# The last product of a two-block network over the listed experts in place of all 16384

## The chip, the cores and the metric

One Trainium2 chip, one core. The metric is the device time of one execution in microseconds (us); lower is better. Engines: PE (TensorE matmul) and PEld (its weight load), DVE (VectorE), ACT (ScalarE), POOL (GpSimd), SP (which here only issues DMAs). PEq, ACTq, SPq and POOLq are the sequencers of these engines.

## The reference

Two transformer blocks on 256 tokens of width 2048, all float32. The first is a convolution mixer and a gated feed-forward; the second is attention with a pooling branch, and then "peer", a layer that picks single-neuron experts. The change concerns only peer:

```
q = (xt @ w_query).reshape(t, 8, 256)            # t = 256 tokens, 8 heads
s1, s2 = q1 . sub_keys_1, q2 . sub_keys_2        # 128 scores each
v1, i1 = top_k(s1, 16);  v2, i2 = top_k(s2, 16)
cand = v1[:, None] + v2[None, :];  top_s, top_pos = top_k(cand, 16)
expert_idx = i1 * 128 + i2 at top_pos;  gates = softmax(top_s)
a   = einsum('thkd,td->thk', expert_u[expert_idx], xb)
out = einsum('thk,thkd->td', gelu(a) * gates, expert_v[expert_idx])
```

So each token weighs 128 of 16384 experts (some may coincide). expert_u and expert_v are 16384 x 2048.

## The kernel before

The kernel doesn't gather. It takes the layer as dense products with a matrix of gates that is zero where an expert wasn't chosen. Expert number e is i * 128 + j, with i on the 128 partitions and j counted in rows of U: row j of the stream holds the experts i * 128 + j for all i. A "half" c is 128 of the 256 tokens.

**Precision.** Each product is three float32r matmuls: both operands are split in a high part (ACT, L69 for streamed weights, L193 for other tiles) and a low part (DVE, L84 and L194), and high x high, high x low and low x high are summed in PSUM.

**Weights.** SP loads all weights in tiles of 128 x 1024 (512 KB), in one order that `stream` writes down (L61). 4 raw tiles (`NRAW`) and 7 split tiles (`NHL`) are in flight; `tick`, called once a row, splits 5 tiles ahead (`LOOK`). A row of U is two such tiles.

**Side work.** `aside(cost, f)` puts work at the end of one list; each `tick` adds `budget` to a credit and takes side work off the front while credit is left.

**The stages of peer.** `query_stage` makes queries and scores and picks the top 16 (`choose`). 128 `gate_step`s, as side work with cost 2.0 at a budget of `BU` = 2.7 a row, each turn two tokens' choices into a 128 x 128 matrix of gates per token: one-hot rows (L1324, L1325) times gates (L1327) on PE (L1332), joined to tile `gch` (L1342). A `gch` of 16 tokens goes to DRAM `gd` by the ACT queue (L1345), 8 KB contiguous for a partition. Beside these, `expert_in` computes the 128 rows of gelu(a) (L187, L1354) and stores each to DRAM `ad`, 1 KB for a partition, again by the ACT queue (L1355); the tile it is stored from has 4 buffers. The last 8 rows (U2) are computed in `expert_out`.

**The last product.** `expert_out` loads gates and gelu(a) for 8 rows at a time (`gin`, L1371; `ain`, L1373; SP queue), multiplies (L1379) and splits them, and multiplies all 128 rows j with the split V, for both halves c and four quarters q of 512 columns: 128 x 2 x 4 x 3 matmuls of 512 columns (L1395 to L1397; some of the last are 256 wide). After each 8 rows `collect` adds the PSUM sums to `acc` in SBUF (L1402). The last sums go out by DMA.

Of the kernel before, what the change touches and what calls it, by code (L numbers as in the profile page):

```python
# [6 lines left out]
F32 = mybir.dt.float32  # L7
# [5 lines left out]
P = 128  # L13
D = 2048
# [23 lines left out]
CH, BU = 4, 2.7  # L38
U1 = 120
ENDS = (0, 0, 512), (1, 0, 256), (1, 256, 256)  # L40
# [55 lines left out]
class Kern:  # L96
    def __init__(self, ctx, tc, A, out):
        self.tc, self.nc, self.A, self.out = tc, tc.nc, A, out
        pool = lambda name, bufs, **k: ctx.enter_context(tc.tile_pool(name=name, bufs=bufs, **k))
        self.pool = pool  # L100
        self.cst = pool("cst", 1)
        self.wraw = pool("wraw", NRAW)
        self.whl = pool("whl", NHL)
        self.tmp = pool("tmp", 3)
        self.small = pool("small", 2)
        self.psA = pool("psA", 5, space=bass.MemoryType.PSUM)
        self.psB = pool("psB", 3, space=bass.MemoryType.PSUM)
# [3 lines left out]
        self.gd = self.dram.tile([P, 16, P, 16], F32, name="gd")  # L111
        self.ad = self.dram.tile([P, P, T], F32, name="ad")
# [175 lines left out]
    def stream(self):  # L288
# [44 lines left out]
        add("V", [A["V"][i] for i in range(P)])  # L333
# [375 lines left out]
    def run(self):  # L709
        nc, tc = self.nc, self.tc  # L710
        self.consts()
        self.stream()
        self.sq = self.cst.tile([P, T], F32, name="sq")
        self.r2 = self.cst.tile([P, T], F32, name="r2")
        silu = self.conv_stage()
        with ExitStack() as late:
            big = self.big = late.enter_context(tc.tile_pool(name="big", bufs=1, reuse_waits="tile"))
            self.ex = late.enter_context(tc.tile_pool(name="ex", bufs=1, reuse_waits="tile"))
            self.t2 = late.enter_context(tc.tile_pool(name="t2", bufs=2, reuse_waits="tile"))
            h = self.bp.tile([P, KD, T], F32, tag="B", name="h")  # L720
# [8 lines left out]
        with ExitStack() as ctx:  # L729
            self.pk = ctx.enter_context(tc.tile_pool(name="pk", bufs=1, reuse_waits="tile"))  # L730
            self.query_stage(xn)
            self.expert_in(xn)
            self.drain()
        self.expert_out(xn, acc)
# [474 lines left out]
    def query_stage(self, xn):  # L1209
        nc = self.nc  # L1210
        pk = self.pk
# [7 lines left out]
        self.sel = [pk.tile([P, 3, P], F32, name=f"sel{c}") for c in range(2)]  # L1219
# [37 lines left out]
    def choose(self, c, val, idx, top, pos, idf):  # L1257

        nc, pk = self.nc, self.pk
# [42 lines left out]
        def turn():  # L1302
# [3 lines left out]
            st = pk.tile([P, 3, P], F32, name=f"selT{c}")  # L1306
            nc.scalar.activation(st.rearrange("p w t -> p (w t)"), ps[:, :3 * P], AF.Copy)
            gh = pk.tile([P, 2, P], F32R, name=f"gh{c}")
# [7 lines left out]
    def gate_step(self, c, st, gh, t0):  # L1316

        nc, pk = self.nc, self.pk
        o1 = pk.tile([P, 2, P], F32R, tag="o1", name=self.nm("o1"), bufs=3)
        oh = pk.tile([P, 2, P], F32, tag="oh", name=self.nm("oh"), bufs=3)  # L1320
        o2 = pk.tile([P, 2, 2, P], F32R, tag="o2", name=self.nm("o2"), bufs=3)
        for u in range(2):
            t = t0 + u
            nc.vector.tensor_scalar(o1[:, u], self.iota, st[:, 0, t:t + 1], None, op0=ALU.is_equal)  # L1324
            nc.vector.tensor_scalar(oh[:, u], self.iota, st[:, 1, t:t + 1], None, op0=ALU.is_equal)  # L1325
            for w in range(2):
                nc.scalar.activation(o2[:, u, w], oh[:, u], AF.Copy, scale=gh[:, w, t:t + 1])  # L1327
# [8 lines left out]
        def ev(ps):  # L1336
            if t0 % 16 == 0:
                self.gch = pk.tile([P, P, 16], F32, tag="gch", name=self.nm("gch"), bufs=2)
# [3 lines left out]
            nc.vector.tensor_tensor(out=self.gch[:, :, t0 % 16:t0 % 16 + 2].rearrange("p j t -> p t j"),  # L1342
                                    in0=v[:, :, 0], in1=t, op=ALU.add)
# [4 lines left out]
    def expert_in(self, xn, second=False):  # L1348
        nc = self.nc

        def ev_a(j, ps):
# [3 lines left out]
            nc.scalar.dma_start(self.ad[j], t)  # L1355
# [6 lines left out]
    def expert_out(self, xn, acc):  # L1362
        nc, tc, W = self.nc, self.tc, self.W
        G = 8
        with ExitStack() as ctx:
            hp = ctx.enter_context(tc.tile_pool(name="hp", bufs=2, reuse_waits="tile"))
            gin, ain, hid = {}, {}, {}

            def load(g):
                gin[g] = hp.tile([P, 16, G, 16], F32, tag="gin", name=f"gin{g}")  # L1370
                nc.sync.dma_start(gin[g], self.gd[:, :, g * G:g * G + G])  # L1371
                ain[g] = hp.tile([P, G, T], F32, tag="ain", name=f"ain{g}")
                nc.sync.dma_start(ain[g], self.ad[g * G:g * G + G].rearrange("j p t -> p j t"))  # L1373

            def mul(g, e):
                if e == 0:
                    hid[g] = hp.tile([P, G, 2 * T], F32R, tag="hid", name=f"hid{g}")
                x = ain[g][:, e]
                nc.vector.tensor_tensor(out=x.rearrange("p (c t) -> p c t", c=16),  # L1379
                                        in0=x.rearrange("p (c t) -> p c t", c=16), in1=gin[g][:, :, e], op=ALU.mult)  # L1380
                self.split(hid[g][:, e], x)
            load(0)
            load(1)
            for e in range(G):
                self.aside(2.6, lambda e=e: mul(0, e))
            self.expert_in(xn, True)
            self.drain()
            tv = self.first["V"]
            def products(ps, g, q, ee, c, o=0, w=512):
                t = tv + ((g * 4 + q) * 2 + ee // 4) * 2 + ee % 4 // 2  # L1390
                W.split_to(t)
                b = ee % 2 * 512 + o
                wh, wl = W.H(t, b, w), W.L(t, b, w)
                xh, xl = hid[g][:, ee, c * P:c * P + P], hid[g][:, ee, T + c * P:T + c * P + P]
                nc.tensor.matmul(ps[:, :w], xh, wh, start=ee == 0, stop=False)  # L1395
                nc.tensor.matmul(ps[:, :w], xh, wl, start=False, stop=False)  # L1396
                nc.tensor.matmul(ps[:, :w], xl, wh, start=False, stop=ee == G - 1)  # L1397
                return t

            def collect(ps, g, q, c, o=0, w=512, dma=nc.sync):  # L1400
                a = acc[:, c, q * 512 + o:q * 512 + o + w]
                nc.vector.tensor_tensor(out=a, in0=a, in1=ps[:, :w], op=ALU.add)  # L1402
                if g == P // G - 1:
                    dma.dma_start(self.out[c * P:c * P + P, q * 512 + o:q * 512 + o + w], a)
            for g in range(P // G):
                for q in range(4):
                    if g == P // G - 1 and q == 3:
                        for i, (c, o, w) in enumerate(ENDS):
                            ps = self.acc()
                            for ee in range(G):  # L1410
                                products(ps, g, q, ee, c, o, w)
                            collect(ps, g, q, c, o, w, nc.scalar if i % 2 else nc.sync)
                        break
                    pss = [self.acc(), self.acc()]
                    for hf in range(2):
                        for e in range(4):
                            for c in range(2):
                                t = products(pss[c], g, q, hf * 4 + e, c)
                        if g + 1 < P // G:
                            self.aside(1.0, lambda g=g, e=q * 2 + hf: mul(g + 1, e))  # L1420
                        if hf == 0:
                            self.tick(t)
                    for c in range(2):
                        collect(pss[c], g, q, c)
                    self.tick(t)
                if g + 2 < P // G:
                    load(g + 2)
            self.drain()
# [12 lines left out]
def lay_out(I):  # L1441
# [39 lines left out]
    o["V"] = I["peer_expert_v_2"][0].reshape(P, 16, 2, 4, 4, 512).transpose(1, 4, 2, 0, 3, 5).reshape(P, P, D)  # L1481
# [29 lines left out]
```

## Time and profile before

| what | us |
|---|---|
| median of 3 runs (lowest, highest) | 3234.52 (3232.54, 3236.83) |
| the profiled execution's own time | 3235.39 |
| its span in the trace | 3233.6 |
| PE busy in the span | 3196.0 (99%) |
| DVE, ACT busy | 2342.8 (72%), 1768.5 (55%) |

The profiled execution is 0.9 us above the median, and has 1.8 us around its span. Matmuls are pipelined, so that PE is "busy" through also where one waits for the array; how far apart matmuls start tells more than the busy share.

### The profile page before, as it was taken

How to read it: one execution, taken by the hardware profiler on the slowest of the kernel's cores; microseconds unless marked ns; L12 is line 12 of the kernel's file. 1: busy time of each engine (PE TensorE's matmuls, PEld its weight loads, DVE VectorE, ACT ScalarE, POOL GpSimd, SP SyncE). 2: the span in 40 equal slices, each digit the busy share in tenths (PEclk: the TensorE clock that was granted, in tenths of full speed). 3: DMA queues.
4: the chain of work that ended last, by engine and by line, in shares of the span. 5: the costliest groups of instructions: out<-in, count | busy, mean ns of one | idle time of the engine just before them, and what ended most of it. 6: DMA issues, size and time to landing. Idle time of an engine off the chain costs nothing.

```text
span 3233.6 us, 47620 instructions
## 1 busy us (share of the span) xinstructions
PE 3196.0 (99%) x17464; PEld 2751.9 (85%) x17464; DVE 2342.8 (72%) x4194; ACT 1768.5 (55%) x3039; POOL 39.8 (1%) x47
## 2 busy tenths in 40 slices
PE   9989999999999999999999999999999999999999
PEld 8978788888888778888888888888888888888888
DVE  8997765666666867776679997777776676666664
ACT  4446644444445645655455567777877444444442
POOL 0110000000000000000000000000000000000000
PEclk9999999999999999999999999999999999999999
DMA  6777465555555555555555667777777977777654
GB/s 207 205 202 218 157 190 189 190 188 188 188 189 189 177 174 182 177 177 189 204 180 195 201 212 226 228 231 235 227 233 228 324 260 246 244 236 247 224 198 154
DMA packets 243995, 672.01 MB, mean 208 GB/s; under 512 B 21920, under 2 KB 95152, under 8 KB 241456
## 3 DMA queue, kind: packets, MB, share of 16 engines
q1 hardware_dynamic: 211968, 616.09, 59.1%
q10 hardware_dynamic: 24832, 41.34, 3.4%
q0 software_dynamic: 6960, 11.54, 2.0%
q8 instruction: 137, 2.24, 0.3%
q14 instruction: 98, 0.80, 0.1%
HBM read 619.58 MB, written 37.77 MB: 203 GB/s over the span
## 4 chain that ended last, share of the span: by engine, by line
PE 89%; DVE 7%; DMA 3%; ACT 1%; issue 1%; SPq 0%; POOL 0%; DVEq 0%; ACTq 0%
PE acc L170 61%; PE acc L1396 7%; PE acc L1395 7%; PE acc L1397 7%; DVE wh L84 2%; DVE conv L471 1%; PE acc L415 1%; DVE acc L471 1%; PE g L1332 1%; DMA wr<-in_w_in_dram 1%; PE acc L940 0%; PE acc L942 0%; PE acc L941 0%; ACT wh L69 0%; DMA cb<-cd 0%
## 5 line engine op out<-in xcount | busy, mean ns | idle before, releaser
L84 DVE TENSOR_TENSOR wh<-wr,wh 128x1024 fp32r<-128x1024 f32 x1062 | 1296.7, 1224 | 730.5 <-ACT wh L69 728.1
L69 ACT ACTIVATE wh<-wr 128x1024 fp32r<-128x1024 f32 x1062 | 1122.9, 1059 | 1220.0 <-PE acc L170 599.1
L170 PE MATMUL acc<-xn,wh 128*128 128x256 f32 x4602 | 822.1, 337 | 0.0
L170 PE MATMUL acc<-n,wh 128*128 128x256 f32 (+1 forms) x4596 | 817.5, 339 | 1.0 <-DVE n L659 1.0
L170 PEld LDWEIGHTS acc<-n,wh 128*128 128x128 f32 x4596 | 703.7, 189 | 109.8 <-issue 5.6
L170 PEld LDWEIGHTS acc<-xn,wh 128*128 128x128 f32 x4602 | 700.5, 188 | 97.6
L1395 PE MATMUL acc<-wh,hid 128*128 128x512 f32 (+1 forms) x1032 | 399.8, 387 | 0.0
L1397 PE MATMUL acc<-wh,hid 128*128 128x512 f32 (+1 forms) x1032 | 399.8, 387 | 0.0
L1396 PE MATMUL acc<-wh,hid 128*128 128x512 f32 (+1 forms) x1032 | 399.8, 387 | 0.0
L170 PE MATMUL acc<-mid,wh 128*128 128x512 f32 (+1 forms) x1386 | 243.2, 337 | 0.0
L170 PEld LDWEIGHTS acc<-mid,wh 128*128 128x128 f32 x1386 | 211.4, 188 | 31.4 <-DVE mid L194 1.1
L1395 PEld LDWEIGHTS acc<-wh,hid 128*128 128x128 f32 x1032 | 193.8, 188 | 39.6
L1396 PEld LDWEIGHTS acc<-wh,hid 128*128 128x128 f32 x1032 | 193.8, 188 | 39.6
L1397 PEld LDWEIGHTS acc<-wh,hid 128*128 128x128 f32 x1032 | 193.8, 188 | 39.6
L1327 ACT ACTIVATE o<-oh,gh 128x128 fp32r<-128x128 f32 x512 | 167.4, 398 | 2.7
L186 ACT ACTIVATE join<-acc 128x256 f32<-128x256 f32 x335 | 121.7, 366 | 3.4 <-PE acc L170 2.7
L415 PE MATMUL acc<-h,wr 128*128 128x272 f32 x448 | 104.9, 392 | 0.0
L415 PEld LDWEIGHTS acc<-h,wr 128*128 128x128 f32 x448 | 84.2, 190 | 16.5
L1324 DVE TENSOR_SCALAR o<-iota,selT 128x128 fp32r<-128x128 f32 x256 | 59.3, 283 | 49.2 <-PE g L1332 48.8
L1402 DVE TENSOR_TENSOR yacc<-yacc,acc 128x512 f32<-128x512 f32 x129 | 82.1, 676 | 14.6 <-PE acc L1397 14.6
L471 DVE SCALAR_TENSOR_TENSOR conv<-up,dw,conv 128x256 f32<-128x256 f32 x180 | 87.4, 485 | 0.0
L170 PE MATMUL acc<-silu,wh 128*128 128x256 f32 (+1 forms) x474 | 83.5, 337 | 0.9 <-DVE silu L194 0.9
(363 smaller groups left out, 2752.4 us busy)
## 6 DMA issues: line engine op xcount, KB each, us to landing
wr<-in_U_dram SPq DMA_DIRECT2D x256, 512.0 KB, 4.6
wr<-in_V_dram SPq DMA_DIRECT2D x256, 512.0 KB, 4.7
wr<-in_gate_dram SPq DMA_DIRECT2D x88, 512.0 KB, 4.4
wr<-in_up_dram SPq DMA_DIRECT2D x88, 512.0 KB, 4.3
wr<-in_down_dram SPq DMA_DIRECT2D x88, 512.0 KB, 4.5
wr<-in_w_out_dram SPq DMA_DIRECT2D x64, 512.0 KB, 4.5
wr<-in_gl_dram SPq DMA_DIRECT2D x64, 512.0 KB, 3.7
wr<-in_w_in_dram SPq DMA_DIRECT2D x63, 512.0 KB, 5.8
```

The source lines that it names most:

```text
L69: self.K.nc.scalar.activation(self.hl[i][:, 0], self.raw[i], AF.Copy)
L84: nc.vector.tensor_tensor(out=h[:, 1], in0=r, in1=h[:, 0].bitcast(F32), op=ALU.subtract)
L170: self.mm = self.nc.tensor.matmul(ps[:, :c], b, x[:, :c], start=first and i == 0, stop=last and i == 1)
L186: nc.scalar.activation(t[:m], ps[:m, n:2 * n], AF.Copy)
L415: nc.tensor.matmul(ps[:, :TM], W.raw[u][:, o:o + P], (hg if i < 4 else h)[:, k], start=k == 0, stop=k == KD - 1)
L471: nc.vector.scalar_tensor_tensor(out=t, in0=x, scalar=w, in1=t, op0=ALU.mult, op1=ALU.add)
L1324: nc.vector.tensor_scalar(o1[:, u], self.iota, st[:, 0, t:t + 1], None, op0=ALU.is_equal)
L1327: nc.scalar.activation(o2[:, u, w], oh[:, u], AF.Copy, scale=gh[:, w, t:t + 1])
L1395: nc.tensor.matmul(ps[:, :w], xh, wh, start=ee == 0, stop=False)
L1396: nc.tensor.matmul(ps[:, :w], xh, wl, start=False, stop=False)
L1397: nc.tensor.matmul(ps[:, :w], xl, wh, start=False, stop=ee == G - 1)
L1402: nc.vector.tensor_tensor(out=a, in0=a, in1=ps[:, :w], op=ALU.add)
```

## The change

Experts are sorted on the chip by which half chose them: only half 0, both, only half 1, none. The first `ND` = 8 rows j stay dense, as before. The 120 x 128 other experts get a place in the sorted order, in blocks of 128: blocks 0 to 24 (`S1`) are taken for half 0 alone, 25 to 76 for both halves, 77 to 104 (`E0` to `E1`) for half 1 alone, 105 to 119 not at all. A flag `more` is set where the counts don't fit these bounds; then all that was left out is computed behind.

- Gates and gelu(a) now share one DRAM tensor `ag`: row (half, expert) of 1 KB, gelu(a) of 128 tokens and then their 128 gates, so that one row gather gets both. A store of gelu(a) is 512 B pieces. A `gch` now holds 32 tokens (`GT`), and its store goes out in pieces of 32 tokens, 128 B, 16384 pieces a store, 8 stores.
- `gate_step` makes both tokens' one-hots in one instruction each; `BU` is 3.5. `use` sums each `gch` over tokens. `classes`, `scan`, `place` (side work) work out the place of each expert, and `scatter` writes the expert numbers to their places in 8 DRAM lists by 120 indirect DMAs of 128 numbers each, on the POOL queue. `read_lists` and `sum_lists` bring them back (a list has zero where another one has the number).
- V is no longer streamed. A block's 128 rows of V (8 KB each) are gathered into a tile of 1 MB by an indirect DMA on the POOL queue, and its rows of `ag` by one more for each half that it is taken for. Dense rows are loaded by SP. 4 buffers of V and of `ag`, 3 of split gates times gelu(a); a block's loads are written 4 and 3 blocks ahead of its products.
- The sums of the eight outputs (2 halves x 4 quarters) stay in all eight PSUM banks through the whole stage; `collect` is called once for each.

```diff
-CH, BU = 4, 2.7
+CH, BU = 4, 3.5
+ND = 8
+NJ = 128 - ND
+S1, E0, E1 = 25, 77, 105
+NLS = 8
+GT = 32
+LV = 4, 3, 2, 2
...
+        self.ag = self.dram.tile([2 * P * P, 2 * P], F32, name="ag")
+        self.agv = self.ag.rearrange("(c i j) t -> c i j t", c=2, i=P)
+        self.ls = [self.dram.tile([P * P, 1], F32, name=f"ls{k}") for k in range(NLS)]
...
-        add("V", [A["V"][i] for i in range(P)])
...
+        for w, o in enumerate((o1, oh)):
+            nc.vector.tensor_tensor(out=o, in0=self.iota.unsqueeze(1).to_broadcast([P, 2, P]),
+                                    in1=st[:, w, t0:t0 + 2].unsqueeze(2).to_broadcast([P, 2, P]), op=ALU.is_equal)
...
-            if t0 % 16 == 14:
-                nc.scalar.dma_start(self.gd[:, c * 8 + t0 // 16], self.gch)
+            if t0 % GT == GT - 2:
+                g = self.gch
+                nc.scalar.dma_start(self.agv[c][:, :, P + t0 + 2 - GT:P + t0 + 2], g)
+                for j in range(0, P, 64):
+                    self.aside(2.2, lambda j=j: use(g, j))
+                if c == 1 and t0 == P - 2:
+                    self.aside(1.5, self.classes)
...
+            for i in range(9):
+                self.aside(0.8, lambda i=i: scan(i))
+            self.aside(2.0, place)
...
+        def scatter():
...
+            for j in range(NJ):
+                nc.gpsimd.indirect_dma_start(self.ls[j % NLS],
+                                             bass.IndirectOffsetOnAxis(ap=self.at[:, j:j + 1], axis=0),
+                                             self.eid[:, ND + j:ND + j + 1], None)
+        self.hook(24, mm)
+
+    def read_lists(self, lb):
+        for k, x in enumerate(self.ls):
+            self.nc.gpsimd.dma_start(lb[:, k], x.rearrange("(p b) o -> p (b o)", p=P))
...
-            nc.scalar.dma_start(self.ad[j], t)
+            nc.scalar.dma_start(self.agv[:, :, j, :P].rearrange("c i t -> i c t"),
+                                t.rearrange("p (c t) -> p c t", c=2))
...
+            def fetch(x):
+                b, cs, listed = x
+                raw[x] = vp.tile([P, D], F32, tag="vr", name=self.nm("vr"), bufs=4)
+                if listed:
+                    nc.gpsimd.indirect_dma_start(raw[x], None, self.A["V"], rows(0, b))
+                else:
+                    nc.sync.dma_start(raw[x], vj[b])
...
+                    for c in cs:
+                        nc.gpsimd.indirect_dma_start(ag[x][:, c], None, self.ag, rows(c, b))
...
+            def prepare_v(x):
...
+                    for o in range(0, D, UW):
+                        h = self.whl.tile([P, 2, UW], F32R, tag="hl", name=self.nm("vh"))
+                        nc.scalar.activation(h[:, 0], r[:, o:o + UW], AF.Copy)
+                        nc.vector.tensor_tensor(out=h[:, 1], in0=r[:, o:o + UW], in1=h[:, 0].bitcast(F32),
+                                                op=ALU.subtract)
...
+            def prepare_hidden(x):
...
+                    nc.vector.tensor_tensor(out=m[:, cs], in0=a[:, cs, :P], in1=a[:, cs, P:], op=ALU.mult)
+                    nc.scalar.activation(h[:, 0, cs], m[:, cs], AF.Copy)
+                    nc.vector.tensor_tensor(out=h[:, 1, cs], in0=m[:, cs], in1=h[:, 0, cs].bitcast(F32),
+                                            op=ALU.subtract)
...
+                for i in range(-LV[0], n):
+                    for f, l in zip((fetch, fetch_hidden, prepare_hidden, prepare_v), LV):
+                        if 0 <= i + l < n:
+                            if f is fetch and i + l == known > 0:
+                                self.sum_lists(lb)
+                            f(seq[i + l])
...
+            v = nc.values_load(self.more, min_val=0, max_val=3)
+            with tc.If(v > 0):
+                for _ in run(rest):
+                    pass
```

`seq`, the order of the blocks, is the 8 dense rows, and then blocks for one half and blocks for both in turn.

## Rows read from the trace of the kernel before

**Rows 1.** The page: span, TensorE's busy time, and the chain that ended last.

```profile
span 3233.6 us, 47620 instructions
...
PE 3196.0 (99%) x17464; PEld 2751.9 (85%) x17464; DVE 2342.8 (72%) x4194; ACT 1768.5 (55%) x3039; POOL 39.8 (1%) x47
...
PE 89%; DVE 7%; DMA 3%; ACT 1%; issue 1%; SPq 0%; POOL 0%; DVEq 0%; ACTq 0%
```

**Rows 2.** Busy time of each engine in three stretches, with clock and DMA share.

```profile
1936.00:2492.00 556.00, 556.00 (x3271) 488.86 (x3270) 422.06 (x905) 432.87 (x1006) 0.00 (x0) 1.00 0.71 229
...
2536.00:2600.00 64.00, 64.00 (x285) 52.97 (x284) 42.26 (x64) 28.72 (x36) 0.00 (x0) 1.00 0.95 311
2600.00:3200.00 600.00, 600.00 (x2649) 496.82 (x2648) 401.92 (x531) 265.72 (x326) 0.00 (x0) 1.00 0.71 233
```

**Rows 3.** Line L1396 alone: durations, first and last start.

```profile
L1396 PE MATMUL acc<-wh,hid x1032: 282/389/389, 2533.8 to 3230.0; 128*128 128x512 f32 x170, 128*128 128x256 f32 x2
```

**Rows 4.** Groups from 2600 to 3200 us: count, busy us, mean ns, idle before.

```profile
L1396 PE MATMUL acc<-wh,hid 128*128 128x512 f32 x883 | 343.5, 389 | 0.0
...
L84 DVE TENSOR_TENSOR wh<-wr,wh 128x1024 fp32r<-128x1024 f32 x224 | 273.5, 1224 | 173.2 <-ACT wh L69 172.7
L69 ACT ACTIVATE wh<-wr 128x1024 fp32r<-128x1024 f32 x222 | 235.5, 1061 | 333.0 <-PE acc L1397 284.1 <-DMA wr<-in_V_dram 41.9 <-DVE ain L1379 3.3
...
L194 DVE TENSOR_TENSOR hid<-ain,hid 128x256 fp32r<-128x256 f32 x104 | 37.1, 419 | 0.0
```

**Rows 5.** The same view from 1936 to 2492 us, beside the gate steps.

```profile
L69 ACT ACTIVATE wh<-wr 128x1024 fp32r<-128x1024 f32 x189 | 200.4, 1060 | 117.8 <-PE acc L170 112.6 <-DMA ad<-a 3.4 <-DVE gch L1342 0.9
L1327 ACT ACTIVATE o<-oh,gh 128x128 fp32r<-128x128 f32 x500 | 163.4, 398 | 2.5
L1342 DVE TENSOR_TENSOR gch<-g,gl 128x256 f32<-128x256 f32 x128 | 72.5, 608 | 0.0
...
L1341 ACT ACTIVATE gl<-g 128x256 f32<-128x256 f32 x127 | 44.8, 378 | 0.9 <-ACT join L186 0.4
```

**Rows 6.** Tile gch: first and last start of its writes and stores.

```profile
L1342 DVE TENSOR_TENSOR gch<-g,gl x128: 591/606/635, 1936.6 to 2491.5; 128x256 f32<-128x256 f32 x128
L1345 ACTq DMA_DIRECT2D gd<-gch x16: 326/444/949, 1967.2 to 2492.4; - x16
```

**Rows 7.** Tile a: first and last start of its stores.

```profile
L1355 ACTq DMA_DIRECT2D ad<-a x128: 326/326/327, 1799.8 to 2540.6; - x128
```

**Rows 8.** DMA queues from 1805 to 1935 us: packets, MB, share of 16 engines.

```profile
q1 hardware_dynamic: 6700, 24.39, 59.4%
q10 hardware_dynamic: 3442, 3.14, 7.0%
```

**Rows 9.** DMA queues from 1940 to 2500 us, with the gate stores in q10.

```profile
q1 hardware_dynamic: 27219, 99.11, 57.2%
q10 hardware_dynamic: 15877, 29.14, 13.7%
```

**Rows 10.** SP's instructions in order of time from 2500 us: start, duration.

```profile
2500.61 0.61 SPq L1371 DMA_DIRECT2D gin<-gd  x1
2501.31 1.35 SPq L1373 DMA_DIRECT2D ain<-ad  x1
2502.72 1.86 SPq L1371 DMA_DIRECT2D gin<-gd  x1
2504.63 5.20 SPq L1373 DMA_DIRECT2D ain<-ad  x1
```

**Rows 11.** POOL's instructions by form.

```profile
L448 POOL DMA_DIRECT2D work<-work x13 | 11.3, 871 | 114.0 <-ACT work L446 114.0
...
L570 POOL DMA_DIRECT2D conv<-r x6 | 7.3, 2461 | 22.0 <-ACT r L568 22.0
```

**Rows 12.** DMA issues: KB of one, median us to landing.

```profile
gin<-gd SPq DMA_DIRECT2D x16, 1024.0 KB, 7.5
...
work<-work POOLq DMA_DIRECT2D x13, 512.0 KB, 9.6
```

More of the change, by code (lines that the diff above doesn't have):

```diff
@@ L1218, in query_stage @@
         idf = [pk.tile([P, 8, 2, 16], F32, name=f"idf{c}") for c in range(2)]
-        self.sel = [pk.tile([P, 3, P], F32, name=f"sel{c}") for c in range(2)]
+        self.sel = [self.pk.tile([P, 3, P], F32, name=f"sel{c}") for c in range(2)]
         NEG = -3.4e38
@@ new lines, in use, with start_lists @@
+        def use(g, j):
+            u = self.used[:, c, j:j + 64]
+            if t0 < GT:
+                nc.vector.tensor_reduce(u, g[:, j:j + 64], axis=mybir.AxisListType.X, op=ALU.add)
+            else:
+                r = self.pg.tile([P, 64], F32, tag="use", name=self.nm("use"), bufs=2)
+                nc.vector.tensor_reduce(r, g[:, j:j + 64], axis=mybir.AxisListType.X, op=ALU.add)
+                nc.vector.tensor_tensor(out=u, in0=u, in1=r, op=ALU.add)
+        mm()
+    def start_lists(self):
+        nc, lp = self.nc, self.lp
+        self.tri = lp.tile([P, P], F32, name="tri")
+        self.eid = lp.tile([P, P], F32, name="eid")
+        for x, a in ((self.tri, "tri"), (self.eid, "eid")):
+            nc.scalar.dma_start(x, self.A[a])
+        self.used = lp.tile([P, 2, P], F32, name="used")
+        self.at = lp.tile([P, NJ], U32, name="at")
+        self.more = lp.tile([1, 1], mybir.dt.int32, name="more")
+        self.lst = lp.tile([P, 2, P], U32, name="lst")
+        z = lp.tile([P, P], F32, name="zero")
+        nc.gpsimd.memset(z, 0.0)
+        for x in self.ls:
+            nc.gpsimd.dma_start(x.rearrange("(p b) o -> p (b o)", p=P), z)
@@ new lines, in read_lists, with sum_lists @@
+    def read_lists(self, lb):
+        for k, x in enumerate(self.ls):
+            self.nc.gpsimd.dma_start(lb[:, k], x.rearrange("(p b) o -> p (b o)", p=P))
+    def sum_lists(self, lb):
+        nc = self.nc
+        n = NLS
+        while n > 2:
+            n //= 2
+            nc.vector.tensor_tensor(out=lb[:, :n], in0=lb[:, :n], in1=lb[:, n:2 * n], op=ALU.add)
+        nc.vector.tensor_tensor(out=lb[:, 0], in0=lb[:, 0], in1=lb[:, 1], op=ALU.add)
+        nc.vector.tensor_copy(self.lst[:, 0], lb[:, 0])
+        nc.vector.tensor_scalar(self.lst[:, 1], lb[:, 0], float(P * P), None, op0=ALU.add)
@@ L1349, in expert_in @@
+    def expert_in(self, xn, second=False, after=None):
         nc = self.nc
@@ L1354, in ev_a @@
             nc.scalar.activation(t, t, AF.Gelu_apprx_tanh)
-            nc.scalar.dma_start(self.ad[j], t)
+            nc.scalar.dma_start(self.agv[:, :, j, :P].rearrange("c i t -> i c t"),
+                                t.rearrange("p (c t) -> p c t", c=2))
+            if after:
+                after(j)
         if not second:
@@ L1362, in expert_out @@
     def expert_out(self, xn, acc):
-        nc, tc, W = self.nc, self.tc, self.W
-        G = 8
-        with ExitStack() as ctx:
[L1366 to L1386, printed above, removed]
-            self.drain()
[L1388 to L1428, printed above, removed]
@@ new lines, in expert_out @@
+        nc, tc = self.nc, self.tc
+        both = (0, 1)
+        one = [(b, (0,), True) for b in range(S1)] + [(b, (1,), True) for b in range(E0, E1)]
+        two = [(b, both, True) for b in range(S1, E0)]
+        seq, k = [(j, both, False) for j in range(ND)], 0
+        for i, x in enumerate(one):
+            seq.append(x)
+            m = (i + 1) * len(two) // len(one)
+            seq += two[k:m]
+            k = m
+        rest = [(b, (0,), True) for b in range(E0, E1)] + [(b, both, True) for b in range(E1, NJ)] + \
+            [(b, (1,), True) for b in range(S1)]
@@ new lines, in expert_out, with fetch_hidden, collect, products @@
+        with ExitStack() as ctx:
+            vp = ctx.enter_context(tc.tile_pool(name="vp", bufs=1, reuse_waits="tile"))
+            lb = vp.tile([P, NLS, P], F32, name="lb")
+            self.read_lists(lb)
+            vj = self.A["V"].rearrange("(i j) d -> j i d", j=P)
+            raw, ag, hl, hid = {}, {}, {}, {}
+            rows = lambda c, b: bass.IndirectOffsetOnAxis(ap=self.lst[:, c, b:b + 1], axis=0)
+            def fetch(x):
[3 more added lines that the diff above has]
+                    nc.gpsimd.indirect_dma_start(raw[x], None, self.A["V"], rows(0, b))
+                else:
+                    nc.sync.dma_start(raw[x], vj[b])
+            def fetch_hidden(x):
+                b, cs, listed = x
+                ag[x] = vp.tile([P, 2, 2 * P], F32, tag="vx", name=self.nm("vx"), bufs=4)
+                if listed:
+                    for c in cs:
+                        nc.gpsimd.indirect_dma_start(ag[x][:, c], None, self.ag, rows(c, b))
+                else:
+                    nc.sync.dma_start(ag[x], self.agv[:, :, b].rearrange("c i t -> i c t"))
+            def prepare_v(x):
+                r, hl[x] = raw.pop(x), []
+                with tc.high_priority(offset=PRIO):
+                    for o in range(0, D, UW):
[3 more added lines that the diff above has]
+                                                op=ALU.subtract)
+                        hl[x].append(h)
+            def prepare_hidden(x):
+                a, cs = ag.pop(x), slice(x[1][0], x[1][-1] + 1)
+                m = vp.tile([P, 2, P], F32, tag="vm", name=self.nm("vm"), bufs=2)
+                h = hid[x] = vp.tile([P, 2, 2, P], F32R, tag="hid", name=self.nm("hid"), bufs=3)
+                with tc.high_priority(offset=PRIO):
+                    nc.vector.tensor_tensor(out=m[:, cs], in0=a[:, cs, :P], in1=a[:, cs, P:], op=ALU.mult)
+                    nc.scalar.activation(h[:, 0, cs], m[:, cs], AF.Copy)
+                    nc.vector.tensor_tensor(out=h[:, 1, cs], in0=m[:, cs], in1=h[:, 0, cs].bitcast(F32),
+                                            op=ALU.subtract)
+            def collect(ps, c, q):
+                a = acc[:, c, q * 512:q * 512 + 512]
+                nc.vector.tensor_tensor(out=a, in0=a, in1=ps, op=ALU.add)
+                (nc.scalar if q % 2 else nc.sync).dma_start(self.out[c * P:c * P + P, q * 512:q * 512 + 512], a)
+            def products(x, pss, first, last):
+                for c in x[1]:
+                    xh, xl = hid[x][:, 0, c], hid[x][:, 1, c]
+                    for q in range(4):
+                        w = hl[x][q // 2]
+                        o = q % 2 * 512
+                        ps = pss[c][q]
+                        for i, (l, r) in enumerate(((xh, 0), (xh, 1), (xl, 0))):
+                            nc.tensor.matmul(ps, l, w[:, r, o:o + 512], start=first[c] == x and i == 0,
+                                             stop=last[c] == x and i == 2)
+                        if last[c] == x:
+                            collect(ps, c, q)
+                del hid[x], hl[x]
+            def run(seq, known=0):
+                first = [[x for x in seq if c in x[1]][0] for c in both]
+                last = [[x for x in seq if c in x[1]][-1] for c in both]
+                n = len(seq)
+                for i in range(-LV[0], n):
[4 more added lines that the diff above has]
+                            f(seq[i + l])
+                    if i == 0:
+                        pss = [[self.acc() if 4 * c + q < 5 else
+                                self.psB.tile([P, 512], F32, tag="b", name=self.nm("out")) for q in range(4)]
+                               for c in both]
+                    if i >= 0:
+                        products(seq[i], pss, first, last)
+                    yield
+            it = run(seq, ND)
+            self.expert_in(xn, True, lambda j: j >= P - LV[0] and next(it))
+            self.drain()
+            for _ in it:
+                pass
+            v = nc.values_load(self.more, min_val=0, max_val=3)
+            with tc.If(v > 0):
+                for _ in run(rest):
+                    pass
```

98 lines of the change are left out of this document (76 added, 22 removed).

## The prediction

> **What bounds the kernel now.** I read the page first: the span, the share of the engines, and the chain of work that ended last. PE fills 99% of the span and 89% of the chain [rows 1]. The busy times by stretch then show that this holds in each stretch that the change touches: PE is busy throughout, at the full clock, beside the gate steps and in the last product [rows 2]. In the last product nothing stands before a matmul (idle before it is 0.0), while DVE waits for ACT and ACT for PE [rows 4]: these two run ahead as far as the buffers let them. So there the time is the number of matmuls times the distance between two. That distance is 600 us / 2649 = 0.2265 us [rows 2], not the 389 ns that one takes, since they overlap [rows 4]. The stage runs from 2533.8 to 3230 us [rows 3].
>
> What the reader is to see besides: DMA is at 0.71 in both stages, and at 0.95 with 311 GB/s where they meet [rows 2]. It is no bound now, but has no large reserve.
>
> **What is removed: matmuls.** Before: 128 x 2 halves x 4 quarters x 3 = 3072 matmuls of 512 columns. After: 8 x 2 + 25 + 28 + 52 x 2 = 173 half-blocks of 12 matmuls, 2076. Removed are 83 half-blocks, 996 matmuls: 996 x 0.2265 = 225.6 us. A half-block then costs 12 x 0.2265 = 2.72 us. `collect` goes from 128 adds to 8 on DVE, which isn't the bound there (402 of 600 us busy [rows 2]): nothing, as PE covers it.
>
> Whether the part behind `more` runs depends on the inputs alone. The reference's own choices on its inputs give, of the listed experts, 3586 for half 0 alone, 6085 for both and 3573 for half 1 alone. The bounds want at least 25 x 128 = 3200, at most 77 x 128 = 9856 (there are 9671), and at most 105 x 128 = 13440 (13244). So it doesn't run.
>
> **What is added, 1: the gate stores.** This is the term that I trust least. Work out what a DMA packet costs on one of the 16 engines. Beside the early rows of U, q10 holds only the stores of gelu(a): 3.14 MB are 3066 packets of 1 KB; 7.0% of 16 x 130 us is 146 us, or 47 ns each [rows 8]. Beside the gate steps q10 takes 13.7% of 16 x 560 us = 1228 us [rows 9]; 94 such stores are 12032 packets or 565 us, and the other 662 us are 16 gate stores of 128 packets of 8 KB: 323 ns each. A line through both is 8 ns + 39 ns per KB: 13 ns for 128 B, 27 ns for 512 B. No row shows a store in pieces of 128 B. The lower bound is the line, 13 ns; the upper is the smallest stored packet that a row shows, 47 ns. I take 20 ns, nearer to the line.
>
> A store is now 16384 packets, 1024 on each engine: 13, 20 or 48 us of all DMA. That could hide, but the issuing engine can't go on. When SP issued two loads of `gin` and two of `ain` at once, (2048 + 1024) x 2 / 16 = 384 packets per engine, the last two issues took 1.86 and 5.20 us, where a `gin` alone takes 0.61 [rows 10]: a queue that is full holds its engine. Until 2509.8 us some 7 us of packets at about 34 ns (two of 27 ns to one of 47) had drained, 210 of 384, so that the queue holds some 150 per engine. Here it is ACT that is held, for (1024 - 150) packets: 11.4, 17.5 or 41 us, and some 2 us for SP's loads in flight. Behind the held ACT stand the high parts of the weights (L69), DVE's low parts behind these, and PE behind both. PE's cover is 5 split tiles of half a row. A row of U takes (2540.6 - 1799.8) / 127 = 5.83 us [rows 7], so the cover is 14.6 us, say 13.5 as the tiles stand on average. PE stalls for 0, 6 or 30 us a store, and for 8 stores 0, 48 or 240 us. I take 48.
>
> The smaller parts of this stage: at 1.75 steps a row in place of 1.35, ACT's busy share goes from 433 of 556 us, 78% [rows 2], by 0.4 x (4 x 0.327 + 0.353) = 0.66 us a row (163.4 / 500 and 44.8 / 127 us [rows 5]) to 89%: PE still covers it, but ACT catches up slowly after a hold. The one-hots are two instructions in place of four; `use` and the scans are DVE work within the budget. The 512 B stores of gelu(a) cost 256 x 27 ns against 128 x 47 ns a row: no difference.
>
> **What is added, 2: the lists.** Check the pace of side work on the kernel before: 128 x 2.0 / 2.7 = 94.8 rows, 553 us, and the steps ran from 1936.6 to 2491.5 [rows 6]. So I trust it for after: 128 x 2.0 + 16 x 2.2 + 1.5 at 3.5 a row is 83.6 rows, the hook 1.5 rows, scans and places 3.2: scatters start 88.3 rows or 515 us after 1936.6, at 2452 (stalls beside the gates shift this and what follows alike). Then 120 scatters stand in line on POOL. The nearest rows are a DMA of 128 rows with 0.87 us on POOL, and one of two tiles with 2.46 [rows 11]. Eight lists are written in turn, each waiting for its last write: at a landing of 9.6 us [rows 12] that is 1.2 us a scatter. I take 1.0 (bounds 0.87 and 2.46): the last is issued at 2572. Then landing and the eight reads behind it on the same queue 12 us, the sum 2, one gather's issue 1, its landing 7.5 as a 1 MB load now [rows 12], the split 1.06 + 1.22 [rows 4]: 25 us, first listed product possible at 2597. PE gets there at 2533.8 + 16 x 2.72 = 2577. Stall: 20 us (5 at 0.87, 196 at 2.46).
>
> **What is moved: V onto POOL's queue.** 105 gathers of V and 157 of `ag` in 157 x 2.72 = 427 us: POOL has 1.63 us for each, more than the 0.87 to 1.2 that I expect. DMA: 105 x 1.049 + 157 x 0.131 = 131 MB in 427 us, 306 GB/s. By packets 13440 x 323 + 20096 x 47 ns over 16 engines is 330 us, 77%; by the stretch with 311 GB/s at 0.95 [rows 2] it would be 400 us, 94%. Both lie below PE, closely. DVE for a pair of blocks, one for one half and one for both: 4 x 1.22 + about 1.4 = 6.3 of 8.15 us. I add 5 us for waits on late gathers (bounds 0 and 40), and 5 for reading the flag and jumping behind the last product, which no row shows (bounds 0 and 15; the last output's DMA covers a part).
>
> **Sum.** 3235.4 - 225.6 + 48 + 20 + 5 + 5 = 3087.8 in the profiled execution's own time; it lay 0.9 above the median, so 3087.
>
> **A rule that speaks against the change.** The Trainium skill, "DMA: Bandwidth & Descriptors", section "Specifications", says that pieces below 512 B make the DMA engine read, modify and write. No row here has such a store, so the trace neither agrees nor disagrees; the third rival below is what it would come to.
>
> **The rivals.**
> 1. No hold worth naming: 13 ns a packet, 0.87 us a scatter. 3235.4 - 225.6 + 0 + 5 + 5 + 0 = 3020. For it: between 1 and 8 KB nearly all of a packet's cost goes with its bytes. Against: eight times 16384 packets where 16 x 128 stood. Chance 0.25 (3010 to 3050).
> 2. My forecast, 3050 to 3130: 0.45.
> 3. A packet of 128 B is read before it is written: twice the line, 26 ns. ACT is held 25 us, PE stalls 11 to 12, 92 us in all: 3235.4 - 225.6 + 92 + 30 = 3132. Chance 0.17 (3130 to 3228).
> 4. POOL becomes the bound: indirect DMAs cost it c each in place of about 1. The product then ends at 2452 + 48 + 25 + 382 c: at c = 2.46 at 3465, slower by 230 us. It decides from c = 1.85, where that is the old end. For it: the form with 2.46 us [rows 11], and that computing addresses is work. Against: 0.87 for the same 128 rows. Chance 0.06. Stores at 47 ns come to 3280 likewise (breaking even near 41 ns): 0.03.
> 5. The change doesn't do what it says and the rest runs too: 83 more half-blocks, 3087 + 226 + some 10 for refilling = 3323. Chance 0.02, as the counts stand.
> No change that can be told (within 0.2%, 6.5 us, about what a measurement of this kernel can tell): 0.02.
>
> **How the numbers follow.** Forecast 3087. Below, nothing that the rows show saves more than the matmuls: 3010. Above I leave out rivals 4 and 5 and the worst part of 3: 3200. Faster: 0.25 + 0.45 + 0.17 = 0.87; same 0.02; slower 0.11.
>
> **What would show it.** In the trace of after: 2076 matmuls in the last product, 0.2265 us apart; long issues of the gate stores on ACT's queue, eight of them, with PE idle behind ACT's high parts late in each; scatters on POOL from about 2450 us plus the stalls; one wait of PE where listed blocks begin; after it PE without gaps. I am wrong if POOL is busy without a pause through the product, if the stores' issue is short (then rival 1), or if PE waits for gathers in every block.

## Result, and the profile of the changed kernel

The changed kernel takes 3185.38 us (median of 4 runs, 3184.19 to 3190.23), the kernel before 3233.53 in the runs beside it: a ratio of 0.9853 [0.9836, 0.987]. It is 1.5% faster, which is clear of the noise, and inside the range, but it gains 48 us where 146 were forecast. The profiled execution took 3184.87.

The first lines of the changed kernel's page, span and busy times:

```profile
span 3183.0 us, 45091 instructions
PE 3003.3 (94%) x16448; PEld 2579.8 (81%) x16448; DVE 2249.3 (71%) x3820; ACT 1733.9 (54%) x2996; POOL 497.0 (16%) x446
```

PE was busy for 99% of the span [rows 1]; now it is for 94%. So matmuls were removed, but PE stands idle somewhere. The busy times by stretch (PE, PEld, DVE, ACT, POOL, granted clock, DMA share, GB/s) say where:

```profile
2050.00:2500.00 450.00, 400.98 (x2220) 342.94 (x2219) 322.04 (x508) 313.37 (x734) 0.00 (x0) 0.93 0.76 199
2500.00:2590.00 90.00, 90.00 (x513) 77.91 (x512) 55.82 (x78) 44.23 (x68) 51.91 (x47) 1.00 0.83 272
2590.00:2700.00 110.00, 24.44 (x123) 20.26 (x121) 7.71 (x13) 7.24 (x11) 75.52 (x82) 0.61 0.06 14
2750.00:3150.00 400.00, 400.00 (x1766) 331.20 (x1766) 290.57 (x396) 233.61 (x295) 307.55 (x245) 1.00 0.87 305
```

Two stretches are short of work: 49 us beside the gate steps, and 86 of the 110 us from 2590 on, where every engine but POOL is nearly idle. In the product PE is full again. PE's waits from 1900 to 2850 us (total, times, longest) name what it waited for:

```profile
PE acc L180 <- DVE wh L92: 84.6, 1, 84.6
PE g L1350 <- ACT o L1345: 46.0, 18, 8.1
```

**The single wait of 84.6 us.** L180 is still the product with U, not yet the product with V. DVE's timeline shows what stood in front of the low part (L92) that PE needed:

```profile
2589.75 0.42 DVE L197 TENSOR_TENSOR a<-acc,join 128x256 f32<-128x256 f32 x1
2689.52 1.15 DVE L1472 TENSOR_TENSOR lb<-lb 128x512 f32<-128x512 f32 x2 [99.36 <-DMA lb<-ls]
2690.59 1.22 DVE L92 TENSOR_TENSOR wh<-wr,wh 128x1024 fp32r<-128x1024 f32 x1
2692.33 1.22 DVE L1538 TENSOR_TENSOR vh<-vr,vh 128x1024 fp32r<-128x1024 f32 x1
```

DVE works in order: the high part for the split at 2690.59 was done on ACT (L77) at 2591.57, and DVE made the low part 99 us later. It waited 99.36 us for the lists at `sum_lists` (L1472), and the last low part of U and every split of V for the dense experts (L1538) stood behind that. What it waited for are the scatters and the reads behind them (instructions on the tile of the lists: shortest, median, longest ns, first and last start):

```profile
L1458 POOL DMA_INDIRECT ls<-eid,at x120: 963/967/1597, 2524.0 to 2682.5; - x120
L1465 POOL DMA_DIRECT2D lb<-ls x8: 535/535/590, 2683.5 to 2687.2; - x8
```

**The 18 waits beside the gates.** The DMAs on the gates' buffer, ACT's and PE's timelines about one of them, and the queues' packets, MB and share from 2050 to 2500 us:

```profile
L1484 ACTq DMA_DIRECT2D ag<-a x128: 366/366/10173, 1800.0 to 2706.7; - x128
L1364 ACTq DMA_DIRECT2D ag<-gch x8: 534/535/587, 1980.8 to 2452.3; - x8
```

```profile
2113.71 0.53 ACTq L1364 DMA_DIRECT2D ag<-gch  x1
2126.15 7.69 ACTq L1484 DMA_DIRECT2D ag<-a  x1
2133.89 0.40 ACT L1345 ACTIVATE o<-oh,gh 128x128 fp32r<-128x128 f32 x1 [7.48 <-issue]
```

```profile
2126.70 2.34 PE L180 MATMUL acc<-xn,wh 128*128 128x512 f32 x6
2135.18 0.58 PE L1350 MATMUL g<-o,o 128*128 128x256 f32 x1 [6.14 <-ACT o L1345]
```

```profile
q1 hardware_dynamic: 18169, 66.17, 45.9%
q10 hardware_dynamic: 132208, 23.07, 29.9%
```

The gate store itself (L1364) issues in 0.53 us. The next DMA on ACT's queue, a store of gelu(a) 12 us later (L1484), is held for 7.69 us, up to 10.17 elsewhere. Behind it stands the one-hot times gate (L1345), and PE waits for that at the gate product (L1350), which stands in PE's order among the matmuls of U. Five of the eight stores make PE wait there for 4.5 us or more; behind the first two the hold is short (2.35 and 1.35 us), and behind the last no gate product is left.

**The product.** Its matmuls (L1565), and POOL's gathers (by form: busy, mean ns, idle before):

```profile
L1565 PE MATMUL acc<-vh,hid x1284: 388/389/767, 2696.7 to 3173.7; 128*128 128x512 f32 x184
L1565 PE MATMUL out<-vh,hid x792: 387/389/628, 2703.1 to 3175.7; 128*128 128x512 f32 x198
```

```profile
L1528 POOL DMA_INDIRECT vx<-ag,lst x157 | 205.9, 1311 | 72.4 <-issue 43.6 <-DVE vm L1547 25.2 <-DMA vx<-ag,lst 3.4
L1519 POOL DMA_INDIRECT vr<-in_V_dram,lst x105 | 120.0, 1142 | 62.6 <-DVE vh L1538 38.1 <-issue 14.3 <-DVE hid L1549 8.2
```

They are 1284 + 792 = 2076, and 400 / 1766 = 0.2265 us apart: both as forecast.

### The profile page after: what moved, and what is told of

Its sections match the earlier page's. It is cut to its first block, busy times and chain, and to the rows that moved or that the text cites. A ratio compares the mean times of both kernels' runs of the same rounds, so it can differ in the third digit from the quotient of the medians.

```text
span 3183.0 us, 45091 instructions
## 1 busy us (share of the span) xinstructions
PE 3003.3 (94%) x16448; PEld 2579.8 (81%) x16448; DVE 2249.3 (71%) x3820; ACT 1733.9 (54%) x2996; POOL 497.0 (16%) x446
## 5 line engine op out<-in xcount | busy, mean ns | idle before, releaser
L92 DVE TENSOR_TENSOR wh<-wr,wh 128x1024 fp32r<-128x1024 f32 x806 | 982.9, 1223 | 550.5 <-ACT wh L77 547.0
L77 ACT ACTIVATE wh<-wr 128x1024 fp32r<-128x1024 f32 x806 | 850.5, 1058 | 816.9 <-PE acc L180 552.4
L180 PE MATMUL acc<-xn,wh 128*128 128x256 f32 x4602 | 849.1, 341 | 87.6 <-DVE wh L92 84.6
L180 PEld LDWEIGHTS acc<-xn,wh 128*128 128x128 f32 x4602 | 708.8, 191 | 185.1 <-DVE wh L92 85.1
L180 PE MATMUL acc<-n,wh 128*128 128x256 f32 (+1 forms) x4596 | 817.2, 339 | 0.0
L180 PEld LDWEIGHTS acc<-n,wh 128*128 128x128 f32 x4596 | 703.9, 189 | 108.1 <-issue 5.6
L1538 DVE TENSOR_TENSOR vh<-vr,vh 128x1024 fp32r<-128x1024 f32 x226 | 271.1, 1220 | 129.1 <-ACT vh L1537 128.6
L1537 ACT ACTIVATE vh<-vr 128x1024 fp32r<-128x1024 f32 x226 | 237.6, 1053 | 164.2 <-PE out L1565 155.8
L1565 PE MATMUL acc<-vh,hid 128*128 128x512 f32 x1284 | 306.7, 390 | 6.2 <-DVE a L197 6.2
L1565 PEld LDWEIGHTS acc<-vh,hid 128*128 128x128 f32 x1284 | 241.2, 188 | 57.2 <-issue 7.3
L1458 POOL DMA_INDIRECT ls<-eid,at x120 | 123.1, 1026 | 857.1 <-DVE at L1455 820.7
L180 PE MATMUL acc<-mid,wh 128*128 128x512 f32 (+1 forms) x1386 | 243.1, 337 | 0.0
L180 PEld LDWEIGHTS acc<-mid,wh 128*128 128x128 f32 x1386 | 211.4, 188 | 31.4 <-DVE mid L204 1.1
L1528 POOL DMA_INDIRECT vx<-ag,lst x157 | 205.9, 1311 | 72.4 <-issue 43.6
L1565 PE MATMUL out<-vh,hid 128*128 128x512 f32 x792 | 195.2, 391 | 0.0
L1345 ACT ACTIVATE o<-oh,gh 128x128 fp32r<-128x128 f32 x512 | 169.2, 394 | 39.2 <-issue 33.7
L1565 PEld LDWEIGHTS out<-vh,hid 128*128 128x128 f32 x792 | 149.6, 189 | 31.3
L1350 PE MATMUL g<-o,o 128*128 128x256 f32 x256 | 78.0, 319 | 46.1 <-ACT o L1345 46.0
```

What stands on the lines that cost most here:

```text
L77: self.K.nc.scalar.activation(self.hl[i][:, 0], self.raw[i], AF.Copy)
L92: nc.vector.tensor_tensor(out=h[:, 1], in0=r, in1=h[:, 0].bitcast(F32), op=ALU.subtract)
L180: self.mm = self.nc.tensor.matmul(ps[:, :c], b, x[:, :c], start=first and i == 0, stop=last and i == 1)
L1350: nc.tensor.matmul(ps[:, u * 2 * P:(u + 1) * 2 * P], o1[:, u], o2[:, u].rearrange("p w j -> p (w j)"), start=True, stop=True)
L1458: nc.gpsimd.indirect_dma_start(self.ls[j % NLS], bass.IndirectOffsetOnAxis(ap=self.at[:, j:j + 1], axis=0), self.eid[:, ND + j:ND + j + 1] ...
L1528: nc.gpsimd.indirect_dma_start(ag[x][:, c], None, self.ag, rows(c, b))
```

## Experiments

Times are medians beside the kernel before (median 3233.0 to 3233.8). Three theories stood for the 98 us that were missing: the wait's place in DVE's order, the scatters' own price, and the size of the hold.

**The lists taken out.** No scatters, no reads, no sums, and the table of experts as it stands in place of the lists, so that V is gathered for other experts:

```diff
-            for j in range(NJ):
-                nc.gpsimd.indirect_dma_start(self.ls[j % NLS],
...
-        nc.vector.tensor_copy(self.lst[:, 0], lb[:, 0])
...
+        nc.vector.tensor_copy(self.lst[:, 0], self.eid)
...
-            self.read_lists(lb)
```

> The 120 scatters and the reads of the lists are left out; the list is the table of expert numbers in its own order, so the gathers fetch as many rows from other places. Theory A (all of the wait of about 90 us where U ends comes from the lists; gathers on POOL keep up): 3185 - 85 - 5 to 10 for the slow start = about 3093. Theory C (gathers set the pace of the last product or cost it at its start): less than 85 us is won.

Measured 3091.59, 0.956 [0.9544, 0.9576]. So the lists cost 3185.4 - 3091.6 = 94 us in all, where the forecast had 20; without them it would have been 3067, so that 25 us are missing elsewhere.

**The wait moved in DVE's order.** `sum_lists` goes behind the dense experts' splits, and the gathers that need the lists one step later:

```diff
-                            if f is fetch and i + l == known > 0:
-                                self.sum_lists(lb)
...
+                    if known > 0 and i == known - 3:
+                        with tc.issue_after(self.low.ins):
+                            self.sum_lists(lb)
+                        fetch(seq[known])
+                        fetch(seq[known + 1])
+                        fetch_hidden(seq[known])
```

> The sums of the lists are put on DVE's queue behind the splits of the last dense row; nothing else is changed. Theory A (DVE stands at the sums 99 us, and the last low part of U2 and all of the dense rows' work stand behind it, so the 8 dense rows cover nothing): the dense rows' 16 x 2.72 = 43 us of products move into the wait; the time falls by about 42 us, from 3185 to some 3143, and PE waits some 50 us once, in front of the first listed block. Theory B (PE waits because the lists are late, wherever the sums stand): no change, 3185.

Measured 3231.23, 0.9998 [0.9989, 1.0008]: a miss. DVE's wait is gone, and another loss is there. PE's waits from 1900 to 2850 us, and a piece of its timeline:

```profile
PE acc L180 <- issue: 105.7, 63, 4.3
```

```profile
2593.25 0.59 PE L180 MATMUL acc<-xn,wh 128*128 128x512 f32 x1 [2.21 <-issue]
2596.05 0.37 PE L180 MATMUL acc<-xn,wh 128*128 128x256 f32 x1 [2.21 <-issue]
2598.85 0.37 PE L180 MATMUL acc<-xn,wh 128*128 128x256 f32 x1 [2.43 <-issue]
2690.55 50.86 PE L180 MATMUL acc<-xn,wh 128*128 128x512 f32 x280 [0.81 <-issue]
```

The profile shows next to nothing that PE waited for, yet from 2543.6 to 2690.5 it starts 90 matmuls, from 2590 on mostly one each 2.80 us, and then 280 in 50.86 us. The scatters run from 2521.8 to 2678.6. I call this the slow issue below.

**The gate stores off ACT's queue**, onto SP's, with the wait where the change has it:

```diff
-                nc.scalar.dma_start(self.agv[c][:, :, P + t0 + 2 - GT:P + t0 + 2], g)
+                nc.sync.dma_start(self.agv[c][:, :, P + t0 + 2 - GT:P + t0 + 2], g)
```

> The eight gate stores are issued by SP in place of ACT, with the same 128 B pieces. Theory A (U loses 73 us because ACT is held by a full queue, and PE stands at the gate matmuls behind ACT): most of it is won, since SP runs 4 raw and 5 split tiles ahead; 3120 to 3145. Theory D (the 131072 small packets take the DMA engines from the weights): no gain, 3185, or a loss.

Measured 3180.37, 0.9828 [0.9802, 0.9854]. The same views as above:

```profile
L1484 ACTq DMA_DIRECT2D ag<-a x128: 365/366/428, 1802.5 to 2705.4; - x128
PE g L1350 <- ACT o L1345: 10.7, 8, 3.1
PE acc L180 <- issue: 105.2, 60, 4.3
```

ACT's hold is gone (428 ns at most in place of 10173). It has moved to SP: a weight load there, 328 ns in the median, now takes up to 13.5 us to issue behind a gate store. The time itself is a miss, as this kernel too has the slow issue.

**The gate stores in large pieces.** They go to another place in DRAM as pieces of 16 KB, still on ACT's queue, and the rows of `ag` get half as long; the output leaves the gates out:

```diff
-                nc.scalar.dma_start(self.agv[c][:, :, P + t0 + 2 - GT:P + t0 + 2], g)
+                nc.scalar.dma_start(self.gs[c * 4 + t0 // GT], g)
```

> The eight gate stores stay on ACT's queue and keep their bytes, but go to a scratch tensor in one piece of 16 KB for a partition; rows of gelu(a) are 512 B, and the hidden values are gelu(a) squared in place of gelu(a) times gates, so the output leaves the gates out. Theories A and D (pieces, held queue or not): U's 73 us are won, about 3112. Theory E (the faster side work itself, at 3.5 a row, overloads ACT and DVE): less than half is won, 3150 or more.

Measured 3163.91, 0.9788 [0.9772, 0.9804]: PE's wait at the gate products is 3.1 us in place of 46.0, and the slow issue costs 104.8. The time alone falls where theory E had it; the two kernels that follow, without a slow issue, decide against E.

**Both, with the lists out as well**, so that no slow issue covers the size of the hold. First with SP's queue (lists out as above), then with large pieces (gates left out as well):

> No scatters and no lists, and gate stores on SP's queue: what U's part loses is seen by itself, against 3092 without lists alone. Theory A (ACT held by the full queue): 3040 to 3055. Theory D (the packets take the DMA engines from the weights): 3085 or more.

> No scatters and no lists, and gate stores in 16 KB pieces on ACT's queue to a scratch tensor (gates left out of the output). Theories A and D: U's 73 us are won, 3020. Theory E (the faster side work is too much for ACT and DVE): 3055 or more.

Measured 3045.70, 0.9416 [0.94, 0.9431], and 3027.74, 0.9366 [0.9351, 0.9382]. Against 3091.6 that is 46 us for the other queue and 64 for the large pieces. With the other queue PE still waits 18.9 us at the gate products; why isn't shown. The stretch from 1936 to 2500 us in the second, then in the kernel with only the lists out:

```profile
1936.00:2500.00 564.00, 559.77 (x3243) 486.46 (x3242) 453.98 (x714) 437.15 (x1002) 0.00 (x0) 1.00 0.74 234
```

```profile
1936.00:2500.00 564.00, 513.44 (x2878) 441.35 (x2878) 416.51 (x658) 407.27 (x960) 0.00 (x0) 0.94 0.78 201
```

In the same time 365 matmuls fewer with the small pieces, at a clock of 0.94 in place of 1.00; at 559.77 / 3243 us each that is 63 of the 64. The shorter rows of `ag` are not what gains: from 2700 to 3000 us both kernels run 1325 matmuls.

**The order and SP's queue together**, and the changed kernel once more:

> Sums of the lists behind the dense rows' splits, and gate stores on SP's queue. If PE issues slowly all through the scatters (theory G, as in the two single edits): the dense rows can't be used as cover, and the time is that of the order alone less the 40 us by which the scatters start earlier, about 3190. If it doesn't: 3185 - 42 - 50 = about 3093.

> The changed kernel once more, as it is. In three of the four kernels before, PE's matmuls of the last rows of U started on a grid of 0.7 us while the scatters ran, with nothing waited for (105 us of it); in the changed kernel's trace they did not. Theory F (that is the program's own): 3185, and no such time. Theory G (it is the scatters' effect on any program here, and comes and goes with the chip or the run): 3185 or some 3225, with that time in the trace.

Measured 3109.46, 0.9614 [0.9595, 0.9634], and 3190.34, 0.9868 [0.9852, 0.9885]. The combination beats both kernels. It has no slow issue, and its wait is now at the first listed block:

```profile
PE acc L1565 <- ACT hid L1548: 58.2, 1, 58.2
```

**What makes the slow issue: a gap in DRAM, and more dense experts.** 4 MB unused in front of the lists with the order alone; then 16 dense experts (`ND = 16`, bounds 24, 72, 98) on order and SP's queue, without and with the gap:

```diff
-ND = 8
+ND = 16
...
+        self.gap = self.dram.tile([P, 8192], F32, name="gap")
```

> The first experiment (sums of the lists behind the dense rows' splits) with 4 MB of unused DRAM put in front of the eight lists; no instruction differs. Theory H (PE's slow issue beside the scatters depends on where the lists lie in DRAM): it goes, and the order gives its 42 us: about 3143. Theory I (it is the program's, not its addresses'): 3231 again.

> Sums behind the dense rows' splits, gate stores on SP's queue, and 16 dense rows in place of 8, with bounds 24, 72 and 98 for the blocks. Against the same with 8 dense rows (3109, PE waiting 58 us before the first listed block): 8 x 5.4 = 43 us more cover and 8 x 1.33 = 11 us fewer scatters, for 178 half-blocks in place of 173, 13.5 us: 3065 to 3072 if PE issues at full speed beside the scatters; some 3150 or more if it falls into the slow issue.

> The kernel before this with 4 MB of unused DRAM in front of the lists. Theory H: the slow issue may come or go against the kernel without the gap; with it 3150 or more, without it 3065 to 3072. Theory I: the same time as without the gap.

Measured for the first 3214.41, 0.9951 [0.9921, 0.9982]; slow issue 78.0 us. The executions of the other two differ too much for a ratio: 3180, 3181, 3126, 3179 and 3181, 3073, 3176, 3160 us, with 86.2 and 85.8 us of slow issue in the profiled ones, which are the first of each. The one of 3073 us lies beside the 3065 to 3072 that were expected without it. That suggests that it changes from one execution to the next of one kernel, but no profile of a short one shows it. The gap doesn't decide it: it is there with the gap in both kernels.

**Scatters kept, nothing waits for them.** The lists are the table of experts, so that V is gathered for other experts; in the second kernel the scatters write rows of 512 B in place of 4 B:

```diff
-        nc.vector.tensor_copy(self.lst[:, 0], lb[:, 0])
...
+        nc.vector.tensor_copy(self.lst[:, 0], self.eid)
...
-            self.read_lists(lb)
```

> The changed kernel with its 120 scatters in place, but its lists are the table of expert numbers, so that DVE waits for nothing (the output uses the wrong experts). Gathers still stand behind the scatters on POOL. Theory K and theory L alike: either PE issues slowly beside the scatters (over 60 us of it in the trace, 3190 to 3230), or it doesn't, and PE waits some 45 us before the first listed block: about 3135.

> The kernel before this, each scatter writing rows of 512 B to a wider scratch tensor in place of 4 B. Theory K (writes of 4 B to DRAM slow PE's issue): no slow issue, about 3135. Theory L (indirect DMAs by POOL do it, whatever they write): as with 4 B.

Measured 3146.74, 0.9733 [0.9717, 0.975], and 3147.13, 0.973 [0.9714, 0.9747], neither with the slow issue. PE's wait in the first:

```profile
PE acc L1559 <- DVE vh L1532: 47.1, 1, 47.1
```

Without the wait 3185.4 - 3146.7 = 39 us are won. That is not its place alone, since the reads and sums are gone too: PE starts the listed blocks 4.6 us after the last scatter's end, and 19.3 us in the kernel with order and SP's queue. The other 3146.7 - 3091.6 = 55 are POOL's: the gathers stand behind the scatters in its order, whether DVE waits for a list or not.

**The combination again:**

> Sums behind the dense rows' splits and gate stores on SP's queue, as before (3109 then). If PE's slow issue comes and goes from load to load, it may now show: 3190. If this program is free of it: 3104 to 3116.

Measured 3103.69, 0.9607 [0.9591, 0.9623]: it holds, near the single prices, 3185.4 - 39 - 46 = 3100. It also prices the wait's place better. Against the kernel with SP's queue and no lists (3045.7) the lists still cost 58 to 64 us here, and 94 where the change has the wait: its place is worth 30 to 36 us.

## Why the prediction was too low, step by step

The sum was 98 us short: 94 - 20 = 74 for the lists, 3091.6 - 3067 = 25 for the gate stores.

**The matmuls removed** are right: 2076 left, 0.2265 us apart.

**The lists are the step that failed, "What is added, 2".** The start of the scatters is right: 2452 plus the 74 us by which U is late (the store of gelu(a) of row 123 starts at 2590.65, before at 2516.54) is 2526, and it was 2524.0. Two things behind it are wrong.
- A scatter was taken at 1.0 us. It is (2682.5 - 2524.0) / 119 = 1.33: 0.97 or more on POOL, and 0.30 us between two. Over 120 that is 39 us. With it, my own step gives the wait as 20 + 39 = 59. That it was 58.2 in the kernel with order and SP's queue is in part luck: there the scatters took 168 us, 48 over the forecast, and a shorter way from them to the first listed product (19 us, not 25) and a later PE (4 us) took 10 back. A landing didn't set the pace: it took 2.2 us, not 9.6.
- I let the dense experts' blocks cover the lists until PE had done them, and didn't ask what stands behind `sum_lists` on DVE. It was the last part of U and the dense blocks' own splits, so they covered nothing, and PE's one wait came not where listed blocks begin but before U had ended. This costs the other 30 to 39.

**The gate stores, "What is added, 1", were mis-sized and put at the wrong place.** The drain is right: ACT's next DMA goes through 20 to 21.5 us after the store, where I had 17.5 + 2. (From 210 drained of 384 packets the queue holds 174, not 150; that is half a us.) But the store's own issue took 0.53 us. By my own sign, a short issue, rival 1 would have held; it didn't, as the hold falls on the next DMA, 10 to 20 us later. And I had PE wait for weights, behind a cover of 13.5 us. It waited at the gate products, which ACT feeds directly and no split tile covers. In 2050 to 2500 us PE is idle for 49.0 us, and its 2220 matmuls are busy for 401 where the rate of the kernel without hold (559.77 / 3243) gives 383. So 49 for waits and 18 that go with a lower clock (0.93 granted; after its pause of 6.14 us a gate product takes PE 0.58 us, and 0.28 before) make 67 of the 74; the other 7 stay open. The store was given 6 us and cost some 9. Large pieces give 64 back, which shows that the pieces cause it: the same 2 MB land in 9.4 us as 128 pieces and in 22.7 as 16384.

**The rule weighed against the change.** By bytes and packets q10 moved x pieces of 128 B and y of 512 B from 2050 to 2500 us: x + y = 132208 and 128 x + 512 y = 23.07 MB give x of about 116,200 and y of about 16,000 (seven stores are 114,688 pieces). They took 29.9% of 16 x 450, 2153 us. With 27 ns for 512 B, 128 B took 14.8 ns (12.1 to 16.7 for the bounds 47 and 13). One store almost by itself says the same: from 2114 to 2134 us q10 moved 16316 packets, 2.09 MB, in 79.9% of 16 x 20 us, 15.7 ns each. That is near the line's 13, and not the doubled 26 of rival 3. A landing is longer than 1024 such packets, which fits the loads that share the engines (45.9% beside the stores). The Trainium skill, "DMA: Bandwidth & Descriptors", section "Specifications", gives a read, modify and write to pieces below 512 B: in these stores of whole 128 B the trace shows no price over the line. They were dear by their number.

**The gathers** are right in what they do to PE: 1.14 and 1.31 us on POOL, the second above the 1.2 that I expected, but both below the 1.63 that there is; 307.55 of 400 us busy, DMA at 305 GB/s and 0.87, which lies between my 0.77 and 0.94. Rival 4 fell, and so did rival 5 by the count of matmuls. Of rival 1 (3020), the kernel with neither hold nor lists is the test: 3027.74.

**The end** took 6.9 us behind the last product where it took 3.2 before: 3.7 where I put 5.

## What to carry to other kernels

Before a wait is put into an in-order engine, list what stands behind it there: work meant to cover the wait covers nothing if its own preparation is queued behind. Price a store by its number of pieces as well as its bytes, look for its hold at the next DMA of its queue, and put it on a queue whose engine has nothing urgent to do next. An edit that shifts two engines' work against each other is worth timing together with others: against the changed kernel the moved wait alone lost 46 us and the other queue alone won 5, both together won 76 and 82.

## What was not expected of the hardware

The slow issue: for 134 to 148 us PE starts 90 to 164 matmuls, where it starts 362 in 63 us beside the scatters of the kernel in which nothing waits for them. In its densest parts it starts one instruction (weight load or matmul) each 1.4 us, and the profile shows next to nothing that it waits for. It begins 20 to 26 us after the first scatter and ends 9 to 13 us after the start of the last; in the three kernels without scatters it never shows. PE idles 78 to 106 us by it, and it is in the profiles of the kernels with the order alone (with the gap too), with either other gate store alone, and with 16 dense experts. It is in neither profile of the changed kernel, where PE runs full for 66 us beside the scatters (2524 to 2590) before it is out of work, nor in those of the combination, nor in those where nothing waits for the scatters.

That it needs the scatters is borne out; what else it needs isn't. Neither the pieces' size (4 and 512 B, both free of it) nor the gap settles it, nor the place of the wait (with the change's own order it is there once the stores are changed). The granted clock is 0.50 (1.2 GHz) in those parts, behind PE's pauses, but a matmul takes 0.37 to 0.59 us then, which makes up little of 2.80. Late loading of code is a rival that no run tests: in these 147 us of the kernel with the order alone the two instruction queues moved one packet each, and the trace doesn't show whether PE waited for more. If it varies between executions of one kernel, as their times suggest, something not fixed by the code takes part. The cause stays open.
